# Attention pairs on TensorE: scores issued together with the values of the pair ahead, and a new order at the end of the output projection

## The chip, the cores and the metric

The kernel runs on one core of a Trainium2 chip. The metric is device time in microseconds (us) of one execution; the figure for a kernel is the median of several executions. TensorE (PE in the profile) has a separate sequencer for weight loads (PEld), which can run beside a matmul; VectorE is DVE, ScalarE is ACT, GpSimd is POOL, and SP issues most DMAs. TensorE works strictly in the order in which its instructions were written.

## The reference

Two layers act on x (256 rows of 1024, float32), with a memory of 256 rows:

```
h = rms_norm(x, norm_g); proj = h @ w_in           # 1024 x 3584
oa = causal attention, 6 heads of 64   (qa, ka: rms_norm and rope)
ob = dilated attention, 6 heads of 64  (three patterns; for 256 rows one mask of log counts)
om = attention on the memory, 4 heads  (mkv = rms_norm(mem) @ w_mem_kv)
y = concat(oa * silu(a_g), ob * silu(b_g), om * silu(m_g))
x = x + y @ w_out                                  # 1024 x 1024
```

Everything is float32. The kernel splits each float32 operand of a large product in a high and a low part (fp32r) and adds three products.

## The kernel before

**Stages.** A layer runs through the projections mkv, mq, mg (memory side), bq, bk, bv, bg (dilated side), aq, ak, av, ag (causal side), and then the output projection. A projection has eight steps over the rows of the weights. The output projection has eight chunks of 128 rows of w_out, taken in the order e = 6, 7 (memory), 3, 4, 5 (dilated), 0, 1, 2 (causal), and four PSUM banks (128 rows of x by 512 columns). One chunk on one bank is called a part here: three matmuls, `out_products` (L658). A chunk e needs `yT[:, e]`, which the pair of heads e makes.

**Pairs of heads.** There are eight pairs in a layer: 0 and 1 of the memory side (e = 6, 7), 2 to 4 of the dilated side (e = 3, 4, 5), 5 to 7 of the causal side (e = 0, 1, 2). `pair_of_heads` (L300) is a generator for one pair. It turns q and k (four transposes), computes the scores of two heads (L319: eight TensorE instructions on half the rows of the array each, written 64*128 in the profile), starts a softmax for each head (`head`, L345; after it three or four transposes, L374, and a copy to pT), computes the values (L336: eight instructions on half the columns, written 128*64), then y (L341), and the two parts of yT (L575, L576). Scores, softmax, transposes and values of a pair depend on each other in that order.

**Order.** The order on TensorE is fixed when the program is written out. A counter `clock` adds an assumed cost for each matmul (L109). After each step of a projection, and after each part, `poll` (L124) resumes the generators whose due time has come. So the work of the pairs stands in visits between steps of the large products. A generator asks to be resumed some units of the counter later (`D_QK` 2.5 after the transposes, `D_SOFTMAX` 5 after the scores, `D_PT` 2.5 after the transposes of the softmax) and `until` puts it off by 0.3 while a condition fails. `live` holds the conditions: scores in the order of pairs with at most three softmax tiles in use, values in the order of pairs with one output bank, and `ready`, which is due times for the projections of the values and of the gates. `finish` (L136) moves the counter on, without any matmul, until a pair is done.

**End of a layer.** `last` (L671) keeps the weights of e = 1 and 2. When the other six chunks are through all banks, each bank takes e = 1 and then e = 2, and is added to x (L682). The next layer's products stand behind this.

Of the kernel before, what the change touches and what calls it, by code (L numbers as in the profile page):

```python
# [16 lines left out]
P = 128  # L17
T = 256
# [13 lines left out]
D_NORM, D_MEM, D_QK, D_SOFTMAX, D_PT, D_EVAC = 8, 1, 2.5, 5, 2.5, 4  # L32
D_FIRST_MEM, D_NEXT_MEM, D_PAIR, D_HEAD = 1, 3, 2, 1
WARM = 7

WHOLE = 2
NEG = -1e30
# [29 lines left out]
def hybrid_kernel(ctx: ExitStack, tc: tile.TileContext, x, mem, mem_t, gains, w_in, w_out, w_mem_kv, qk_g, const, out):  # L67
# [73 lines left out]
    def until(cond):  # L141
        while not cond():
            yield 0.3
# [125 lines left out]
    def normed(accs, n, dsts, tables, scale=None):  # L269
# [25 lines left out]
                                            op=ALU.mult))  # L295
        return rest

    live = dict(pr=0, pT=0, o=0, heads=0, pairs=0, s=0, t=0, v=0)

    def pair_of_heads(qn, kn, pair, masks, v, gate, ready, finished):  # L300

        ps = work()
        for t in range(NT):
            transpose(ps[:, t * P:(t + 1) * P], qn[:, t, pair * P:(pair + 1) * P])
            transpose(ps[:, 256 + t * P:256 + (t + 1) * P], kn[:, t, pair * P:(pair + 1) * P])
        qkT = sp.tile([P, 2, T], F32, tag="qkT", name="qkT", bufs=SLOTS)
        nc.scalar.copy(qkT.rearrange("p c t -> p (c t)"), ps)
        me = live["pairs"]
        live["pairs"] += 1
        yield D_QK  # L310
        yield from until(lambda: live["s"] == me and live["pr"] + 2 <= PR_BUFS)
        live["s"] += 1
        live["pr"] += 2
        scores = [work() for _ in range(2)]
        spans = [slice(0, 2 * P), slice(2 * P, 4 * P)] if masks is None else [slice(0, P), slice(P, 3 * P)]
        for t in range(NT):
            for j in range(2):
                q, k = (qkT[j * HD:(j + 1) * HD, c] for c in range(2))
                mm(scores[j][:, spans[t]], q[:, t * P:(t + 1) * P], k[:, 0:spans[t].stop - spans[t].start])  # L319
        pTs = []  # L320
        for j in range(2):
            rest = head(2 * me + j, scores[j], spans, masks, pTs)
            spawn(rest, next(rest))
        yield D_SOFTMAX
        yield from until(lambda: len(pTs) == 2)
        yield D_PT
        yield from until(lambda: live["v"] == me and live["o"] < O_BUFS and max(ready.values()) <= clock[0])
        live["v"] += 1
        live["o"] += 1
        o = o_p.tile([P, T], F32, tag="o", name="o")  # L330
        late = slice(0, T) if masks is None else slice(P, T)
        n = 2 * T if masks is None else T + P
        for t, to in ((0, slice(0, T)), (1, late)):
            for j in range(2):
                h = 2 * pair + j
                mm(o[j * HD:(j + 1) * HD, to], v[:, t, h * HD:(h + 1) * HD], pTs[j][:, t * T:n if t else T],  # L336
                   start=t == 0, stop=t == 1, shared=j)
        live["pT"] -= 2
        yield 0.6
        y = sp.tile([P, T], F32, tag="y", name="y", bufs=2)  # L340
        nc.vector.scalar_tensor_tensor(y, o, 0.5, gate[:, pair], op0=ALU.mult, op1=ALU.mult)  # L341
        live["o"] -= 1
        finished(y)

    def head(me, s, spans, masks, pTs):  # L345

        pr = sp.tile([P, 512], F32, tag="pr", name="pr", bufs=PR_BUFS)
        nm = sp.tile([P, NT], F32, tag="nm", name="nm", bufs=4)
        sums = sp.tile([P, NT], F32, tag="sums", name="sums", bufs=4)
        if masks is None:  # L350
            nc.vector.tensor_reduce(nm, s.rearrange("p (t k) -> p t k", t=NT), axis=AX.X, op=ALU.max, negate=True)
            for t in range(NT):
                nc.scalar.activation(pr[:, spans[t]], s[:, spans[t]], AF.Exp, bias=nm[:, t:t + 1],
                                     accum_out=sums[:, t:t + 1])
            blocks = [0, 2 * P, P, 3 * P]
        else:
            for t in range(NT):
                nc.vector.tensor_tensor_reduce(out=pr[:, spans[t]], in0=s[:, spans[t]], in1=masks[t], scale=-1.0,  # L358
                                               scalar=3e38, op0=ALU.add, op1=ALU.min, accum_out=nm[:, t:t + 1])
                nc.scalar.activation(pr[:, spans[t]], pr[:, spans[t]], AF.Exp, scale=-1.0, bias=nm[:, t:t + 1],  # L360
                                     accum_out=sums[:, t:t + 1])
            blocks = [0, P, 2 * P]
        rinv = sp.tile([P, NT], F32, tag="rinv", name="rinv", bufs=4)
        nc.vector.reciprocal(rinv, sums)
        for t in range(NT):
            nc.scalar.activation(pr[:, spans[t]], pr[:, spans[t]], AF.Copy, scale=rinv[:, t:t + 1])  # L366
        yield D_SOFTMAX + D_HEAD * (me % 2)
        yield from until(lambda: live["t"] == me and live["pT"] < PT_BUFS)
        live["t"] += 1
        live["pT"] += 1  # L370
        n = P * len(blocks)
        ps = work()
        for i, c in enumerate(blocks):
            transpose(ps[:, i * P:(i + 1) * P], pr[:, c:c + P])  # L374
        live["pr"] -= 1
        pT = sp.tile([P, 512], F32, tag="pT", name="pT", bufs=PT_BUFS)
        nc.scalar.copy(pT[:, :n], ps[:, :n])  # L377
        pTs.append(pT)
# [122 lines left out]
    for l in range(DEPTH):  # L501
# [71 lines left out]
        def finished(y, e, yT=yT, done=done):  # L573
            done.add(e)
            nc.scalar.copy(yT[0][:, e], y)  # L575
            nc.vector.tensor_tensor(yT[1][:, e], y, yT[0][:, e].bitcast(F32), op=ALU.subtract)  # L576

        def start_heads(pairs, e0, qn, kn, masks, v, gate, ready, delay=D_NORM):
            for pair in range(pairs):
                spawn(pair_of_heads(qn, kn, pair, masks, v, gate, ready,  # L580
                                    lambda y, e=e0 + pair: finished(y, e)), delay + D_PAIR * pair)


        qn, kn, kv, gate = head_tiles(256, 512)
# [46 lines left out]
        for kind, e0 in ((2, 3), (0, 0)):  # L631
            if kind == 2:
                masks = [cst[:, C_DIL:C_DIL + 128], cst[:, C_DIL + 128:C_DIL + 384]]
            else:
                masks = [cst[:, C_CAUSAL + 128:C_CAUSAL + 256], cst[:, C_CAUSAL:C_CAUSAL + 256]]
            if l + 1 < DEPTH and kind == 0:
                mem_xs = xm_tiles()
                spawn(next_mem(mem_xs, gT[:, 24 + 8 * l:32 + 8 * l]), D_FIRST_MEM)
            qn, kn, v, gate = head_tiles(384, 384)
            ready = dict(v=1e9, gate=1e9)  # L640
            for i, dst in ((0, qn), (1, kn)):
                accs = run(project(xs, weights(), 384))
                normed(accs, 384, [dst[:, t] for t in range(NT)],
                       [[tab[:, kind + i, c, t] for t in range(NT)] for c in range(2)])()
            start_heads(3, e0, qn, kn, masks, v, gate, ready)
            for t, acc in enumerate(run(project(xs, weights(), 384))):
                nc.scalar.copy(v[:, t], acc)
            ready["v"] = clock[0] + D_EVAC
            gates(run(project_t(xs, weights(), 256)), gate[:, 0:2])
            gates(run(project_t(xs, weights(), 128)), gate[:, 2:3])  # L650
            ready["gate"] = clock[0] + D_EVAC


        whole_banks = [(t, c, 512) for t in range(NT) for c in (0, 512)]
# [8 lines left out]
        for c in ("om", "ob", "oa"):  # L663
            for k, _, w in weights():
                e = e_rows[c][0] + k
                finish(lambda: e in done)
                if c == "om" and k == 0:
                    banks = {(t, half): acc_p.tile([P, 512], F32, tag="acc", name="acc")
                             for t in range(NT) for half in range(2)}
                if e in (1, 2):  # L670
                    last.append((e, w))  # L671
                    continue
                for part in whole_banks:
                    out_products(e, w, *part)
                    poll()
        for t, c, n in whole_banks:
            for e, w in last:
                out_products(e, w, t, c, n)
            step = n // 2 if l == DEPTH - 1 and (t, c) == whole_banks[-1][:2] else n
            for a in range(c, c + n, step):  # L680
                cols = slice(a, a + step)
                nc.vector.tensor_tensor(x_sb[:, t, cols], banks[t, c // 512][:, a % 512:a % 512 + step],  # L682
                                        x_sb[:, t, cols], op=ALU.add)
                if l == DEPTH - 1:
                    nc.sync.dma_start(out[t * P:(t + 1) * P, cols], x_sb[:, t, cols])
# [30 lines left out]
```

## Time and profile before

| | us |
|---|---|
| median of three executions | 292.31 (291.97 to 292.39) |
| the profiled execution | 292.05 |
| its span, first to last instruction | 290.3 |
| outside the span | 1.75 |
| TensorE busy | 285.2 of 290.3 |

The granted clock of TensorE is 1.00 in the whole span, its higher level. Times in the rows are in us from the start of the span. A row of the timeline has the start, the length from the first start to the last end, the engine, the line, the operation and how many instructions are merged in it; the end of a matmul is modelled and reaches into the next one, so the price of a piece of work is read from start to start.

### The profile page before, as it was taken

How to read it: one execution, taken by the hardware profiler on the slowest of the kernel's cores; microseconds unless marked ns; L12 is line 12 of the kernel's file. 1: busy time of each engine (PE TensorE's matmuls, PEld its weight loads, DVE VectorE, ACT ScalarE, POOL GpSimd, SP SyncE). 2: the span in 40 equal slices, each digit the busy share in tenths (PEclk: the TensorE clock that was granted, in tenths of full speed). 3: DMA queues.
4: the chain of work that ended last, by engine and by line, in shares of the span. 5: the costliest groups of instructions: out<-in, count | busy, mean ns of one | idle time of the engine just before them, and what ended most of it. 6: DMA issues, size and time to landing. Idle time of an engine off the chain costs nothing.

```text
span 290.3 us, 4972 instructions
## 1 busy us (share of the span) xinstructions
PE 285.2 (98%) x1810; PEld 250.7 (86%) x1810; DVE 205.2 (71%) x461; ACT 200.1 (69%) x446; POOL 54.3 (19%) x72
## 2 busy tenths in 40 slices
PE   8999999999999999999999999999999999999994
PEld 5799999889989999877788999989899899987773
DVE  1798999793677996764676577979655699765313
ACT  2899678876789638985367555868578865698600
POOL 0003993200003220000020069503000113000000
PEclk9999999999999999999999999999999999999999
DMA  7999575627335237538025828360913624920003
GB/s 234 391 368 365 211 214 166 168 56 269 111 93 163 71 121 250 215 143 288 2 76 181 252 76 230 135 183 0 325 31 105 231 64 153 342 74 21 3 0 145
DMA packets 32793, 47.33 MB, mean 163 GB/s; under 512 B 1280, under 2 KB 27648, under 8 KB 32768
## 3 DMA queue, kind: packets, MB, share of 16 engines
q1 hardware_dynamic: 32336, 46.22, 48.6%
q10 hardware_dynamic: 432, 0.79, 0.8%
q8 instruction: 14, 0.23, 0.3%
q14 instruction: 11, 0.09, 0.1%
HBM read 45.96 MB, written 1.05 MB: 162 GB/s over the span
## 4 chain that ended last, share of the span: by engine, by line
PE 97%; DMA 1%; DVE 0%; SPq 0%; DVEq 0%; issue 0%
PE acc L110 79%; PE wk L113 8%; PE wk L110 5%; PE o L110 5%; DMA memT<-in_mem_t_dram 1%; PE o L113 0%; DVE x_sb L682 0%; SPq L469 0%; DVE whole L515 0%; DVEq L712 0%; DVEq L515 0%
## 5 line engine op out<-in xcount | busy, mean ns | idle before, releaser
L450 DVE TENSOR_TENSOR lo<-raw,hi 128x768 fp32r<-128x768 f32 (+1 forms) x90 | 95.6, 1088 | 30.8 <-ACT hi L449 30.7
L449 ACT CAST hi<-raw 128x768 fp32r<-128x768 f32 (+1 forms) x90 | 82.9, 935 | 30.8 <-PE acc L110 22.9
L110 PE MATMUL acc<-hi,xmh 128*128 128x384 f32 (+2 forms) x252 | 67.4, 349 | 0.0
L110 PE MATMUL acc<-lo,xmh 128*128 128x384 f32 (+2 forms) x252 | 63.7, 335 | 0.0
L110 PE MATMUL acc<-hi,xml 128*128 128x384 f32 (+2 forms) x252 | 63.7, 335 | 0.0
L155 POOL TENSOR_TENSOR hrs<-ms,mhalf 128x6 f32<-128x6 f32 (+1 forms) x24 | 30.1, 1260 | 118.1 <-DVE ms L154 117.6
L110 PEld LDWEIGHTS acc<-hi,xmh 128*128 128x128 f32 x252 | 42.6, 189 | 5.0 <-issue 3.3
L110 PEld LDWEIGHTS acc<-lo,xmh 128*128 128x128 f32 x252 | 45.0, 188 | 1.2
L110 PEld LDWEIGHTS acc<-hi,xml 128*128 128x128 f32 x252 | 44.9, 188 | 1.1
L110 PE MATMUL acc<-hi,yT 128*128 128x512 f32 x128 | 41.0, 402 | 0.0
L110 PE MATMUL acc<-xmh,hi 128*128 128x256 f32 x128 | 29.7, 293 | 0.0
L110 PE MATMUL acc<-xml,hi 128*128 128x256 f32 x128 | 28.4, 283 | 0.0
L110 PE MATMUL acc<-xmh,lo 128*128 128x256 f32 x128 | 28.4, 283 | 0.0
L110 PEld LDWEIGHTS acc<-hi,yT 128*128 128x128 f32 x128 | 23.0, 188 | 4.8 <-issue 0.7
L360 ACT ACTIVATE pr<-pr,nm 128x128 f32<-128x128 f32 (+1 forms) x48 | 21.3, 446 | 7.8 <-DVE nm L358 7.8
L366 ACT ACTIVATE pr<-pr,rinv 128x128 f32<-128x128 f32 (+1 forms) x64 | 25.8, 463 | 0.0
L110 PE MATMUL acc<-lo,yT 128*128 128x512 f32 x64 | 25.0, 391 | 0.0
L110 PEld LDWEIGHTS acc<-xmh,hi 128*128 128x128 f32 x128 | 20.9, 191 | 0.7 <-issue 0.7
L110 PEld LDWEIGHTS acc<-xml,hi 128*128 128x128 f32 x128 | 21.0, 191 | 0.0
L110 PEld LDWEIGHTS acc<-xmh,lo 128*128 128x128 f32 x128 | 21.0, 191 | 0.0
L377 ACT COPY pT<-wk 128x384 f32<-128x384 f32 (+1 forms) x32 | 15.5, 503 | 5.9 <-PE wk L113 5.9
L358 DVE CUSTOM_DVE_ANT_0 pr<-wk,cst 128x128 f32<-128x128 f32 (+1 forms) x48 | 14.3, 353 | 3.3 <-PE wk L110 3.3
(83 smaller groups left out, 357.6 us busy)
## 6 DMA issues: line engine op xcount, KB each, us to landing
raw<-in_w_in_dram SPq DMA_DIRECT2D x24, 768.0 KB, 5.3
raw<-in_w_in_dram SPq DMA_DIRECT2D x7, 1024.0 KB, 5.5
raw<-in_w_out_dram SPq DMA_DIRECT2D x6, 1024.0 KB, 5.0
raw<-in_w_in_dram SPq DMA_DIRECT2D x6, 512.0 KB, 3.7
raw<-in_w_out_dram SPq DMA_DIRECT2D x4, 512.0 KB, 4.0
raw<-in_w_mem_kv_dram SPq DMA_DIRECT2D x2, 1024.0 KB, 5.3
raw<-in_w_mem_kv_dram SPq DMA_DIRECT2D x2, 512.0 KB, 6.8
x_sb<-in_x_dram SPq DMA_DIRECT2D x2, 512.0 KB, 7.3
```

Source lines behind the costliest of these rows:

```text
L110: pe(nc.tensor.matmul(out, a, b, start=start, stop=stop), us)
L113: pe(nc.tensor.transpose(out, a, ident), 0.109)
L155: pin(nc.gpsimd.tensor_tensor(dst, ms, mhalf[:, :n], op=ALU.pow))
L358: nc.vector.tensor_tensor_reduce(out=pr[:, spans[t]], in0=s[:, spans[t]], in1=masks[t], scale=-1.0, scalar=3e38, op0=ALU.add, op1=ALU.min, ...
L360: nc.scalar.activation(pr[:, spans[t]], pr[:, spans[t]], AF.Exp, scale=-1.0, bias=nm[:, t:t + 1], accum_out=sums[:, t:t + 1])
L366: nc.scalar.activation(pr[:, spans[t]], pr[:, spans[t]], AF.Copy, scale=rinv[:, t:t + 1])
L377: nc.scalar.copy(pT[:, :n], ps[:, :n])
L449: pin(nc.scalar.copy(hi, raw))
L450: pin(nc.vector.tensor_tensor(lo, raw, hi.bitcast(F32), op=ALU.subtract))
```

## The change

A pair that has its pT no longer issues its values at once. It puts a function into `pending`, and waits until the next pair takes it, the next pair has issued its scores, or 14 units have passed. The next pair, once it may issue its scores, waits up to 5 units for a pending pair ahead (on the dilated and causal sides except the last causal pair; not on the memory side but for its first pair), issues its scores, and then the pending values right behind them. The last causal pair (`alone`, e = 2) doesn't wait, and its delays are 1.5 and 1 units shorter. The due time of the gates is no condition for the values any more. In the output projection the program no longer waits for e = 1 and 2 when their weights are taken; the end goes through banks 0, 1, 2 with e = 1, then banks 0, 1, 2 with e = 2, then bank 3 with both, and waits for each e only there, polling after each part.

```diff
--- before.py
+++ after.py
@@ -32,6 +32,7 @@
 D_NORM, D_MEM, D_QK, D_SOFTMAX, D_PT, D_EVAC = 8, 1, 2.5, 5, 2.5, 4
 D_FIRST_MEM, D_NEXT_MEM, D_PAIR, D_HEAD = 1, 3, 2, 1
 WARM = 7
+D_PARTNER, D_SCORES = 5, 14
 
 WHOLE = 2
 NEG = -1e30
@@ -295,9 +296,10 @@
                                             op=ALU.mult))
         return rest
 
+    pending = {}
     live = dict(pr=0, pT=0, o=0, heads=0, pairs=0, s=0, t=0, v=0)
 
-    def pair_of_heads(qn, kn, pair, masks, v, gate, ready, finished):
+    def pair_of_heads(qn, kn, pair, masks, v, gate, ready, finished, alone):
 
         ps = work()
         for t in range(NT):
@@ -309,6 +311,8 @@
         live["pairs"] += 1
         yield D_QK
         yield from until(lambda: live["s"] == me and live["pr"] + 2 <= PR_BUFS)
+        late = clock[0] + (D_PARTNER if masks is not None and not alone or pair == 0 else 0)
+        yield from until(lambda: live["v"] >= me or me - 1 in pending or clock[0] >= late)
         live["s"] += 1
         live["pr"] += 2
         scores = [work() for _ in range(2)]
@@ -318,31 +322,45 @@
                 q, k = (qkT[j * HD:(j + 1) * HD, c] for c in range(2))
                 mm(scores[j][:, spans[t]], q[:, t * P:(t + 1) * P], k[:, 0:spans[t].stop - spans[t].start])
         pTs = []
+        if me - 1 in pending:
+            pending.pop(me - 1)()
         for j in range(2):
-            rest = head(2 * me + j, scores[j], spans, masks, pTs)
+            rest = head(2 * me + j, scores[j], spans, masks, pTs, D_SOFTMAX - 1.5 * alone)
             spawn(rest, next(rest))
-        yield D_SOFTMAX
+        yield D_SOFTMAX - 1.5 * alone
         yield from until(lambda: len(pTs) == 2)
-        yield D_PT
+        yield D_PT - alone
         yield from until(lambda: live["v"] == me and live["o"] < O_BUFS and max(ready.values()) <= clock[0])
-        live["v"] += 1
-        live["o"] += 1
-        o = o_p.tile([P, T], F32, tag="o", name="o")
-        late = slice(0, T) if masks is None else slice(P, T)
-        n = 2 * T if masks is None else T + P
-        for t, to in ((0, slice(0, T)), (1, late)):
-            for j in range(2):
-                h = 2 * pair + j
-                mm(o[j * HD:(j + 1) * HD, to], v[:, t, h * HD:(h + 1) * HD], pTs[j][:, t * T:n if t else T],
-                   start=t == 0, stop=t == 1, shared=j)
-        live["pT"] -= 2
+        outs = []
+
+        def values():
+            live["v"] += 1
+            live["o"] += 1
+            o = o_p.tile([P, T], F32, tag="o", name="o")
+            late = slice(0, T) if masks is None else slice(P, T)
+            n = 2 * T if masks is None else T + P
+            for t, to in ((0, slice(0, T)), (1, late)):
+                for j in range(2):
+                    h = 2 * pair + j
+                    mm(o[j * HD:(j + 1) * HD, to], v[:, t, h * HD:(h + 1) * HD], pTs[j][:, t * T:n if t else T],
+                       start=t == 0, stop=t == 1, shared=j)
+            live["pT"] -= 2
+            outs.append(o)
+
+
+        pending[me] = values
+        late = clock[0] + (0 if alone else D_SCORES)
+        yield from until(lambda: outs or live["s"] > me + 1 or clock[0] >= late)
+        if not outs:
+            pending.pop(me)()
+        o = outs[0]
         yield 0.6
         y = sp.tile([P, T], F32, tag="y", name="y", bufs=2)
         nc.vector.scalar_tensor_tensor(y, o, 0.5, gate[:, pair], op0=ALU.mult, op1=ALU.mult)
         live["o"] -= 1
         finished(y)
 
-    def head(me, s, spans, masks, pTs):
+    def head(me, s, spans, masks, pTs, delay):
 
         pr = sp.tile([P, 512], F32, tag="pr", name="pr", bufs=PR_BUFS)
         nm = sp.tile([P, NT], F32, tag="nm", name="nm", bufs=4)
@@ -364,7 +382,7 @@
         nc.vector.reciprocal(rinv, sums)
         for t in range(NT):
             nc.scalar.activation(pr[:, spans[t]], pr[:, spans[t]], AF.Copy, scale=rinv[:, t:t + 1])
-        yield D_SOFTMAX + D_HEAD * (me % 2)
+        yield delay + D_HEAD * (me % 2)
         yield from until(lambda: live["t"] == me and live["pT"] < PT_BUFS)
         live["t"] += 1
         live["pT"] += 1
@@ -578,7 +596,7 @@
         def start_heads(pairs, e0, qn, kn, masks, v, gate, ready, delay=D_NORM):
             for pair in range(pairs):
                 spawn(pair_of_heads(qn, kn, pair, masks, v, gate, ready,
-                                    lambda y, e=e0 + pair: finished(y, e)), delay + D_PAIR * pair)
+                                    lambda y, e=e0 + pair: finished(y, e), e0 + pair == 2), delay + D_PAIR * pair)
 
 
         qn, kn, kv, gate = head_tiles(256, 512)
@@ -637,7 +655,7 @@
                 mem_xs = xm_tiles()
                 spawn(next_mem(mem_xs, gT[:, 24 + 8 * l:32 + 8 * l]), D_FIRST_MEM)
             qn, kn, v, gate = head_tiles(384, 384)
-            ready = dict(v=1e9, gate=1e9)
+            ready = dict(v=1e9)
             for i, dst in ((0, qn), (1, kn)):
                 accs = run(project(xs, weights(), 384))
                 normed(accs, 384, [dst[:, t] for t in range(NT)],
@@ -648,7 +666,6 @@
             ready["v"] = clock[0] + D_EVAC
             gates(run(project_t(xs, weights(), 256)), gate[:, 0:2])
             gates(run(project_t(xs, weights(), 128)), gate[:, 2:3])
-            ready["gate"] = clock[0] + D_EVAC
 
 
         whole_banks = [(t, c, 512) for t in range(NT) for c in (0, 512)]
@@ -663,7 +680,8 @@
         for c in ("om", "ob", "oa"):
             for k, _, w in weights():
                 e = e_rows[c][0] + k
-                finish(lambda: e in done)
+                if e not in (1, 2):
+                    finish(lambda: e in done)
                 if c == "om" and k == 0:
                     banks = {(t, half): acc_p.tile([P, 512], F32, tag="acc", name="acc")
                              for t in range(NT) for half in range(2)}
@@ -673,9 +691,15 @@
                 for part in whole_banks:
                     out_products(e, w, *part)
                     poll()
-        for t, c, n in whole_banks:
-            for e, w in last:
-                out_products(e, w, t, c, n)
+        ends = [(b, i) for i in range(2) for b in range(3)] + [(3, 0), (3, 1)]
+        for b, i in ends:
+            t, c, n = whole_banks[b]
+            e, w = last[i]
+            finish(lambda: e in done)
+            out_products(e, w, t, c, n)
+            poll()
+            if i == 0:
+                continue
             step = n // 2 if l == DEPTH - 1 and (t, c) == whole_banks[-1][:2] else n
             for a in range(c, c + n, step):
                 cols = slice(a, a + step)
```

## Rows read from the trace of the kernel before

**Rows 1.** Busy time of each engine in two stretches, from the first full matmul to the end of the last: us of the stretch, then busy us and instructions of each engine, granted clock, DMA share, GB/s.

```profile
4.70:153.00 148.30, 148.29 (x925) 129.29 (x926) 113.81 (x249) 110.95 (x242) 29.30 (x36) 1.00 0.57 190
153.00:286.60 133.60, 133.59 (x873) 118.36 (x871) 90.13 (x207) 87.66 (x202) 24.31 (x30) 1.00 0.41 133
```

**Rows 2.** Timeline of TensorE around scores that stand alone between steps (first layer, pair 2).

```profile
67.49 0.40 PE L110 MATMUL acc<-xmh,lo 128*128 128x256 f32 x2
67.81 0.93 PE L110 MATMUL wk<-qkT 64*128 64x128 f32 x8
68.67 0.50 PE L110 MATMUL acc<-xmh,hi 128*128 128x256 f32 x2
69.01 0.40 PE L110 MATMUL acc<-xml,hi 128*128 128x256 f32 x2
69.25 0.40 PE L110 MATMUL acc<-xmh,lo 128*128 128x256 f32 x2
```

**Rows 3.** Timeline of TensorE around values that stand alone (first layer, pair 2).

```profile
80.70 0.51 PE L110 MATMUL acc<-hi,xml 128*128 128x384 f32 x2
81.05 0.51 PE L110 MATMUL acc<-lo,xmh 128*128 128x384 f32 x2
81.49 0.87 PE L110 MATMUL o<-pT,v 128*64 128x256 f32 x8
82.29 0.62 PE L110 MATMUL acc<-hi,xmh 128*128 128x384 f32 x2
82.75 0.51 PE L110 MATMUL acc<-hi,xml 128*128 128x384 f32 x2
```

**Rows 4.** Timeline of the weight loads of TensorE, second layer: values, the product behind them, scores, and the product behind those. In brackets is the idle time of the loader before the row.

```profile
221.44 0.63 PEld L110 LDWEIGHTS o<-pT,v 128*64 128x64 f32 x8 [0.25 <-issue]
222.24 0.30 PEld L110 LDWEIGHTS acc<-hi,xmh 128*128 128x128 f32 x2 [0.17 <-issue]
225.19 0.52 PEld L110 LDWEIGHTS wk<-qkT 64*128 64x128 f32 x8 [0.25 <-issue]
226.05 0.30 PEld L110 LDWEIGHTS acc<-hi,xmh 128*128 128x128 f32 x2 [0.33 <-issue]
```

**Rows 5.** Timeline of TensorE in the output projection of the first layer: values (pair 5) with transposes behind them, then scores (pair 7) with transposes behind them.

```profile
123.94 0.39 PE L110 MATMUL acc<-lo,yT 128*128 128x512 f32 x1
124.26 0.87 PE L110 MATMUL o<-pT,v 128*64 128x256 f32 x8
125.06 0.55 PE L113 MATMUL wk<-ident,pr 128*128 128x128 f32 x3
...
125.91 0.40 PE L110 MATMUL acc<-lo,yT 128*128 128x512 f32 x1
126.24 0.93 PE L110 MATMUL wk<-qkT 64*128 64x128 f32 x8
127.09 0.55 PE L113 MATMUL wk<-ident,pr 128*128 128x128 f32 x3
...
127.94 0.39 PE L110 MATMUL acc<-lo,yT 128*128 128x512 f32 x1
```

**Rows 6.** The same timeline later: one full part (two rows) and the start of the next, and three transposes that stand alone.

```profile
128.17 0.61 PE L110 MATMUL acc<-hi,yT 128*128 128x512 f32 x2
128.63 0.39 PE L110 MATMUL acc<-lo,yT 128*128 128x512 f32 x1
128.85 0.61 PE L110 MATMUL acc<-hi,yT 128*128 128x512 f32 x2
...
133.07 0.40 PE L110 MATMUL acc<-lo,yT 128*128 128x512 f32 x1
133.31 0.49 PE L113 MATMUL wk<-ident,pr 128*128 128x128 f32 x3
133.56 0.71 PE L110 MATMUL acc<-hi,yT 128*128 128x512 f32 x2
134.11 0.40 PE L110 MATMUL acc<-lo,yT 128*128 128x512 f32 x1
```

**Rows 7.** Timeline of TensorE, the scores of pair 4 in the first layer and in the second.

```profile
85.24 1.11 PE L110 MATMUL wk<-qkT 64*128 64x128 f32 x8
...
225.19 0.93 PE L110 MATMUL wk<-qkT 64*128 64x128 f32 x8
```

**Rows 8.** Timeline of all engines at the end of the second layer, where the last pair becomes yT.

```profile
277.98 0.87 PE L110 MATMUL o<-pT,v 128*64 128x256 f32 x8
...
278.78 0.74 PE L110 MATMUL acc<-hi,yT 128*128 128x512 f32 x2
278.90 0.42 DVE L341 SCALAR_TENSOR_TENSOR y<-o,gate 128x256 f32<-128x256 f32 x1 [5.32 <-PE o L110]
...
279.36 0.41 ACT L575 CAST yT<-y 128x256 fp32r<-128x256 f32 x1 [4.22 <-DVE y L341]
...
279.79 0.42 DVE L576 TENSOR_TENSOR yT<-y,yT 128x256 fp32r<-128x256 f32 x1 [0.47 <-ACT yT L575]
```

**Rows 9.** The same at the end of the first layer, where weights of the next layer are still split.

```profile
138.48 1.23 DVE L450 TENSOR_TENSOR lo<-raw,hi 128x1024 fp32r<-128x1024 f32 x1 [1.86 <-ACT hi L449]
138.99 0.30 PEld L110 LDWEIGHTS acc<-hi,yT 128*128 128x128 f32 x2 [0.17 <-issue]
...
139.62 0.42 DVE L341 SCALAR_TENSOR_TENSOR y<-o,gate 128x256 f32<-128x256 f32 x1
...
140.51 0.43 DVE L576 TENSOR_TENSOR yT<-y,yT 128x256 fp32r<-128x256 f32 x1 [0.47 <-ACT yT L575]
141.17 1.05 ACT L449 CAST hi<-raw 128x1024 fp32r<-128x1024 f32 x1 [0.69 <-PE acc L110]
```

**Rows 10.** Timeline of ACT after the scores of pair 7, first layer: the first exponential, and the four scalings that end the softmax of both heads.

```profile
127.53 0.40 ACT L360 ACTIVATE pr<-pr,nm 128x128 f32<-128x128 f32 x1 [0.15 <-DVE nm L358]
...
129.66 1.50 ACT L366 ACTIVATE pr<-pr,rinv 128x128 f32<-128x128 f32 x4
```

**Rows 11.** Timeline of ACT in the second layer: the last cast of a weight in the program.

```profile
270.84 1.04 ACT L449 CAST hi<-raw 128x1024 fp32r<-128x1024 f32 x1
```

## The prediction

> **What bounds the kernel now.** I read the busy time by stretch first. From 4.70 to 286.60 us TensorE is busy in 281.88 of 281.90 us [rows 1], at the full granted clock. So there is no data wait to remove, and nothing on DVE, ACT or the DMA queues matters unless it makes TensorE wait. What can move the time is TensorE's own cost, and the reader should look for time in which it passes as busy and does little. The weight loader shows it: in the steps of the large products it runs ahead, but it stands idle 0.25 us before the weights of scores or values, 0.33 us after scores and 0.17 us after values [rows 4]. These are the places where the array goes from 128*128 to a half-row or half-column shape or back. So each visit pays twice for the change of shape, beside its work. The price of a visit is read from start to start. Two 256-column matmuls take 0.24 us [rows 2], two of 384 columns 0.35 [rows 3], and two of 512 columns 0.46, with 0.68 for a part [rows 6]. Lone scores: the product before ends at 67.49 + 0.24 = 67.73, the one behind is at normal pace from 69.01 - 0.24 = 68.77, so they cost 1.04. Lone values: 82.75 - 0.35 - (81.05 + 0.35) = 1.00.
>
> **The order after the change.** No arithmetic is added or removed; only the order changes. I walked the generators by hand with the costs of L109 (used for the order alone). The walk gives each visit of before where the trace has it, for example the values of pair 5 seven parts into the output projection, held by the gates' due time. For after it gives in each layer:
> - Pair 1's values wait for pair 2's scores, during bg: one visit, with the transposes of pair 4 behind. Pair 3's scores wait five steps, from the end of bg into aq, until pair 2's values are pending: one visit. Likewise 3 with the scores of 4, 4 with the scores of 5 (the transposes of pair 7 behind), 5 with the scores of 6 after the sixth part. Five shared visits in a layer, ten in all.
> - Pair 7's scores go alone after part 15 (before: part 8), since the scores of 6 came later. Pair 6's values follow after part 20, alone, with both transposes of pair 7's softmax right behind. Pair 7's values follow after part 24 (before: part 21). So `finish` never moves the counter without work: e = 1 is done by part 21, e = 2 in the poll after the first part of e = 1.
>
> **What a shared visit saves.** Entry 0.08 (67.73 to 67.81), scores up to the next shape 0.85 (126.24 to 127.09 [rows 5]), values up to the next shape 0.80 (81.49 to 82.29), and 0.11 for refilling behind (82.29 to 82.75 is 0.46 where 0.35 is normal): 1.84 against 1.04 + 1.00 = 2.04. It saves 0.20. No row has scores followed by values. From below, the step from one to the other might cost no change of shape, which would spare some 0.2 more; from above, it might cost as much as the two changes that it replaces, and save nothing. I take the row that I have, scores followed by another shape, 0.85. The loader's idle time after scores (0.33) and before values (0.25) shows TensorE emptying at each change of shape. The Trainium skill, TensorEngine Tiling (Array Packing), section Key Properties, says the same: changing the tiling mode, not just the tile, drains TensorE. Row tiling to column tiling is such a change, so the rule speaks against a larger gain: one of four drains goes, not two.
>
> **Shared edges that are lost.** Some visits of before already border on transposes, which have the shape of the large products. Three transposes alone cost 134.11 - 0.46 - (133.07 + 0.23) = 0.35 [rows 6]. Values with three cost 125.91 - 0.46 - (123.94 + 0.23) = 1.28, so 0.07 less than apart; scores with three cost 127.94 - 0.46 - (125.91 + 0.23) = 1.34, 0.05 less. The scores of pair 3 lose such an edge (0.05), and in the visit of pairs 6 and 5 both lose one (0.12). The values of pair 1 and the scores of pair 5 had an edge, and their shared visits have one behind them again. The sum for a layer: 5 x 0.20 - 0.05 - 0.12 = 0.83, and + 0.10 for pair 6's values, which gain the edge and put six transposes in one run (0.07, and one re-entry of about 0.03): 0.93. Two layers: 1.86. The scores of pair 4 took 1.11 us in the first layer and 0.93 in the second [rows 7]: 0.18 of waiting behind the transposes of pair 3's softmax, one step earlier. These will now be four steps earlier, so the wait should go. Sum 2.04.
>
> **What is added.** TensorE now gets yT of e = 2 much later, and everything behind it in its queue (the rest of the end, then the next layer's mkv) waits if it is late. Its cover is three parts of e = 1, 3 x 0.68 = 2.04, and 0.11. In the second layer yT is whole at 279.79 + 0.42 = 280.21, 1.43 after TensorE left the values at 278.78 [rows 8]: hidden. If the cover were gone, it would cost these 1.43. In the first layer a split of the next layer's weights stands in front on DVE, and it took 140.51 + 0.43 - 138.99 = 1.95: just hidden. But the cast of the buffer that chunk e = 0 frees (141.17 in before [rows 9]) will now fall into the same moment, and its DVE half takes 1.23; in front of y it makes 1.43 + 1.23 = 2.66, up to 0.6 late. Bounds 0 and 0.6; I take 0.2, nearer to the row of the first layer, which is hidden. The earlier transposes of pair 7 are asked for 0.31 (its neighbour's transposes) + 5 x 0.68 + 0.09 + 0.90 = 4.7 us after its scores left TensorE. In before the first head's scalings were over 129.66 + 0.75 - 127.09 = 3.3 after, the second's at 4.1 [rows 10]: hidden, with about 1 us, the length of one cast. Values of pairs 1 to 4 come up to 12 us later or sooner, but their chunks are taken tens of us after; the later scores of pair 3 (4.5 us) push its softmax and nothing on TensorE, since the transposes' due times move with it. The bank adds of the end come nearer together, but the last bank is unchanged, and so is the tail behind it. The gates' due time falls out: the gates are written before the values in all cases of the walk. SP and POOL are not touched.
>
> **Sum.** 2.04 - 0.20 = 1.84 saved. The profiled execution, 292.05, would take 290.2; on the median, 0.26 above it, 290.5. I say 290.4.
>
> **Rivals.**
> - The step from scores to values costs as much as the two changes that it replaces. Then ten merges give nothing, the lost edges stay: -2 x (0.17 - 0.10) + 0.18 - 0.20 = -0.16, so about 292.5. For it: both shapes are partial, and no row shows them together. Against it: all changes seen cost much the same. 0.08. The same time comes out if the merges don't come about because due times miss; each miss costs 0.2 only, and the walk has one margin under 0.1 unit (pair 5 after part 6), worth 0.4 over both layers, which stays in the forecast.
> - The step needs no emptying, since the loader works on tiles beside each other: 10 x 0.2 more, 288.5. The skill's rule above is against it, and so is the equal idle time at each change. 0.05.
> - Slower: e = 2 is late. The end waits for yT behind casts on ACT and DVE, in both layers. It decides from a chain of 2.15 us on, and it makes the kernel slower only if it eats the 2.04 of the sum and 0.6 more, 1.3 us per layer, that is yT 3.5 us after the values. That is 1.43 and two casts of about 1.1. In the second layer no cast is left by then (the last is at 270.84 [rows 11]), which speaks against it; the shortened delays of the last pair could add to it, with a late softmax. 293.0. 0.06.
>
> **How the numbers follow.** The forecast has 0.81, with its own range 289.6 to 291.4: the bounds of the wait (0 to 0.6), half of either bound for the step. For 8 in 10 the range goes from 289.3 to 291.9; the rivals, 0.19, lie outside. About 0.2%, 0.58 us, is what a measurement can tell from no change. Faster by more than that is below 291.7: the forecast and the second rival, less a little of the forecast's upper end, 0.84. Same: the first rival and that end, 0.10. Slower 0.06.
>
> **What would show it.** The trace should have ten places where 64*128 is followed by 128*64 with no 128*128 between, the second starting about 0.85 after the first; the loader's idle time on issue should be less by one 0.25 for each. TensorE should stay busy from 4.7 us to the end. The walk is wrong if the values of pair 7 don't come 24 parts into the output projection. The forecast is wrong if the first part of e = 2 waits on DVE or ACT, if transposes after pair 6's values wait on ACT, or if the step from scores to values is near 0.65 or 1.05.

## The result, and the profile after

The changed kernel took 290.00 us (median of six, 289.74 to 290.69) where the kernel before took 292.03 beside it (291.47 to 292.39): ratio 0.9936, 95% interval 0.9920 to 0.9953, so 1.4 to 2.3 us less. The forecast was 290.4, with 1.84 saved. The profiled execution took 289.94, with a span of 288.1. Single executions far above the others (351 us in e2, 562 us in e7) are left out of the times below.

Busy time by stretch, columns as in [rows 1]:

```profile
4.70:152.00 147.30, 146.47 (x926) 129.07 (x927) 114.40 (x250) 110.22 (x242) 29.19 (x36) 1.00 0.58 192
152.00:284.50 132.50, 132.49 (x871) 118.40 (x869) 90.51 (x207) 87.28 (x202) 23.49 (x30) 1.00 0.41 132
```

TensorE is still always busy and at full clock; the 0.83 us missing in the first stretch lie at its start, where it waited for VectorE, and VectorE for the first DMA. So the time came out of busy time. The timeline of TensorE in the output projection of the first layer shows where: a shared visit, pair 6's scores with pair 5's values.

```profile
120.95 0.39 PE L111 MATMUL acc<-lo,yT 128*128 128x512 f32 x1
121.27 0.93 PE L111 MATMUL wk<-qkT 64*128 64x128 f32 x8
122.12 0.87 PE L111 MATMUL o<-pT,v 128*64 128x256 f32 x8
122.92 0.74 PE L111 MATMUL acc<-hi,yT 128*128 128x512 f32 x2
123.50 0.39 PE L111 MATMUL acc<-lo,yT 128*128 128x512 f32 x1
```

The values start 0.85 after the scores, the same as transposes did [rows 5], and the product follows 0.80 later, as after lone values [rows 3]. The whole visit costs 123.50 - 0.46 - (120.95 + 0.23) = 1.86; 1.84 was forecast, and apart they cost 2.04. In all ten shared visits the values start 0.85 or 0.86 after the scores. The loader's rows in the second layer (scores, values, product of the shared visit of pairs 3 and 2) answer to [rows 4]:

```profile
219.04 0.52 PEld L111 LDWEIGHTS wk<-qkT 64*128 64x128 f32 x8 [0.25 <-issue]
219.90 0.63 PEld L111 LDWEIGHTS o<-pT,v 128*64 128x64 f32 x8 [0.33 <-issue]
220.70 0.30 PEld L111 LDWEIGHTS acc<-hi,xmh 128*128 128x128 f32 x2 [0.17 <-issue]
```

Where four idle times stood (0.25, 0.33, 0.25, 0.17), there are three: one entry is gone.

The end of the first layer answers to [rows 9], here with the parts of TensorE:

```profile
138.79 0.87 PE L111 MATMUL o<-pT,v 128*64 128x256 f32 x8
139.59 0.74 PE L111 MATMUL acc<-hi,yT 128*128 128x512 f32 x2
139.71 0.42 DVE L359 SCALAR_TENSOR_TENSOR y<-o,gate 128x256 f32<-128x256 f32 x1 [1.35 <-PE o L111]
140.05 1.22 DVE L468 TENSOR_TENSOR lo<-raw,hi 128x1024 fp32r<-128x1024 f32 x1
...
141.18 0.42 DVE L594 TENSOR_TENSOR yT<-y,yT 128x256 fp32r<-128x256 f32 x1
...
141.79 0.63 PE L111 MATMUL acc<-hi,yT 128*128 128x512 f32 x2
```

Three parts of e = 1 start at 139.59, 140.41 and 141.10; the first of e = 2 starts at 141.79, without a wait. The split of the next layer's weights did fall into this moment, but behind y: it stood between y and the second half of yT, and yT was whole at 141.60, just in time.

The scores of pair 4 take 0.93 in the first layer too, where they took 1.11 [rows 7]:

```profile
92.85 0.93 PE L111 MATMUL wk<-qkT 64*128 64x128 f32 x8
```

For the sums below I cut every trace at the same work: the first scores of each layer (pair 0), and the add of the last bank. In the changed kernel these are the rows

```profile
39.90 0.73 PEld L111 LDWEIGHTS wk<-qkT 64*128 64x128 f32 x8 [0.25 <-issue]
...
178.79 0.73 PEld L111 LDWEIGHTS wk<-qkT 64*128 64x128 f32 x8 [0.25 <-issue]
```

```profile
284.52 0.76 DVE L706 TENSOR_TENSOR x_sb<-acc,x_sb 128x256 f32<-128x256 f32 x2 [0.67 <-PE acc L111]
```

The same work in the kernel before starts at 40.27, 180.23 and 286.63. "First" is from the first mark to the second, "second" from there to the third, both read in the one profiled execution of each kernel. Ratios are to executions of the kernel before that ran beside the kernel of the row.

| kernel | to the first mark | first | second | sum | ratio to before (95%) |
|---|---|---|---|---|---|
| before | 40.27 | 139.96 | 106.40 | 246.36 | 1 |
| changed | 39.90 | 138.89 | 105.73 | 244.62 | 0.9936 (0.9920 to 0.9953) |
| e8, the changed kernel again | 41.24 | 138.89 | 105.52 | 244.41 | 0.9927 (0.9898 to 0.9956) |
| e1, values one step after the scores | 41.15 | 140.45 | 106.57 | 247.02 | 1.0039 (1.0027 to 1.0052) |
| e2, the old end | 40.31 | 140.23 | 106.07 | 246.30 | 1.0024 (1.0002 to 1.0045) |
| e3, no sharing | 39.87 | 140.54 | 107.02 | 247.56 | 1.0033 (1.0016 to 1.0049) |
| e4, scores don't wait | 40.62 | 139.40 | 106.02 | 245.42 | 0.9961 (0.9949 to 0.9974) |
| e9, usual delays for the last pair | 41.14 | 140.22 | 106.86 | 247.08 | 1.0014 (0.9997 to 1.0032) |
| e6, all seven visits shared | 40.25 | 140.26 | 106.34 | 246.60 | 1.0027 (1.0016 to 1.0038) |
| e7, memory pairs shared, + 2.5 | 40.09 | 142.13 | 107.06 | 249.19 | 1.0103 (1.0068 to 1.0139) |
| e10, memory pairs shared, + 1.2 | 39.92 | 138.69 | 105.33 | 244.02 | 0.9909 (0.9882 to 0.9936) |

The stretch to the first mark is the same program in all of them and spreads by 1.4 us, so it can't be put down to the change; TensorE waits there for data of the first DMAs. The layers repeat: 138.89 in both traces of the changed kernel. The 0.21 between its second layers is one wait inside the scores of memory pair 1 (1.35 us long, 1.13 in e8), which came once.

### The profile page after: what moved, and what is told of

It is laid out like the page before. It is cut to its first block, busy times and chain, and to the rows that moved or that the text cites. A ratio compares the mean times of both kernels' runs of the same rounds, so it can differ in the third digit from the quotient of the medians.

```text
span 288.1 us, 4967 instructions
## 1 busy us (share of the span) xinstructions
PE 282.3 (98%) x1810; PEld 250.5 (87%) x1810; DVE 205.9 (71%) x461; ACT 199.0 (69%) x446; POOL 53.4 (19%) x72
## 3 DMA queue, kind: packets, MB, share of 16 engines
HBM read 45.96 MB, written 1.05 MB: 163 GB/s over the span
## 4 chain that ended last, share of the span: by engine, by line
PE 97%; DMA 1%; DVE 0%; SPq 0%; DVEq 0%; issue 0%
PE acc L111 79%; PE wk L114 8%; PE wk L111 5%; PE o L111 5%; DMA memT<-in_mem_t_dram 1%; PE o L114 0%; DVE x_sb L706 0%; SPq L487 0%; DVE whole L533 0%; DVEq L736 0%; DVEq L533 0%
## 5 line engine op out<-in xcount | busy, mean ns | idle before, releaser
L111 PE MATMUL acc<-hi,xmh 128*128 128x384 f32 (+2 forms) x252 | 66.6, 346 | 0.0
```

Source lines behind the costliest of these rows:

```text
L111: pe(nc.tensor.matmul(out, a, b, start=start, stop=stop), us)
```

## The experiments

Theory A is the prediction's: each shared visit spares one change of the array's shape. Theory B: the gain comes from the rest of the change, the new end of the layer and the sooner last pair. Sums are compared with e8's 244.41.

**e8_changed_again.** The changed kernel itself. 

> The changed kernel itself, beside the two others on one chip. Both theories: ratio to before 0.992 to 0.995. The spans from the first scores of one layer to the first of the next should repeat to a few hundredths of a us (138.9), while the stretch ahead of the first scores, which waits on the first DMAs, may differ by half a us or more.

It came out so: 290.18 us, with 138.89 for the first layer.

**e1_apart.** The values a step later, everything else as changed:

```diff
         pTs = []
-        if me - 1 in pending:
-            pending.pop(me - 1)()
```

> The values of the pair ahead come one step (or part) after the scores instead of right behind them; all waits, the new end and the order of everything else stay. Theory A (each shared visit spares one of four changes of the array's shape, about 0.2 us): all ten are lost, and the sixes of transposes split into threes; some 2.0 us slower than the changed kernel, about as the kernel before (ratio to before 0.998 to 1.002). Theory B (the gain comes from the other places: last pair sooner, end of the layer, values later): the time stays at the changed kernel's, ratio 0.993 to 0.995.

It took 292.84 us; the ratio, 1.0039, is a little above the range of theory A. The same visit as above, now with a part between (TensorE, first layer):

```profile
121.95 0.93 PE L111 MATMUL wk<-qkT 64*128 64x128 f32 x8
122.81 0.73 PE L111 MATMUL acc<-hi,yT 128*128 128x512 f32 x2
123.38 0.40 PE L111 MATMUL acc<-lo,yT 128*128 128x512 f32 x1
123.70 0.87 PE L111 MATMUL o<-pT,v 128*64 128x256 f32 x8
124.50 0.73 PE L111 MATMUL acc<-hi,yT 128*128 128x512 f32 x2
```

From the scores to the product behind the values it is 2.55, and with sharing 1.65 plus a part of 0.68: 0.22 lost by the step between alone. The second layer is 1.05 longer than e8's, five times 0.21. The first is 1.56 longer, but has a wait beside it: its six transposes behind pair 6's values run from 135.43 to 136.71, 0.65 longer than the changed kernel's (135.21 to 135.84):

```profile
135.43 1.53 PE L114 MATMUL wk<-ident,pr 128*128 128x128 f32 x6
136.71 0.71 PE L111 MATMUL acc<-hi,yT 128*128 128x512 f32 x2
```

So 0.91 there without the wait, and 1.96 in both layers, where some 2.0 was expected. The wait has the cause told under e3. The adjacency is worth 0.2 us a visit, with the rest of the order unchanged. This shows theory A.

Is it the change of shape that costs, or any break in the row of large products? The transposes have the full shape, and the changed kernel has six of them behind values:

```profile
134.09 0.39 PE L111 MATMUL acc<-lo,yT 128*128 128x512 f32 x1
134.41 0.87 PE L111 MATMUL o<-pT,v 128*64 128x256 f32 x8
135.21 0.88 PE L114 MATMUL wk<-ident,pr 128*128 128x128 f32 x6
135.84 0.71 PE L111 MATMUL acc<-hi,yT 128*128 128x512 f32 x2
136.39 0.40 PE L111 MATMUL acc<-lo,yT 128*128 128x512 f32 x1
```

That visit costs 136.39 - 0.46 - (134.09 + 0.23) = 1.61, and values with three transposes cost 1.28 [rows 5]. So three more cost 0.33 in the same run, and 0.35 as a visit of their own [rows 6]: a break without a change of shape costs 0.02, a tenth of what a shared visit spares.

**e3_end_only.** No sharing, the rest of the change kept:

```diff
-        late = clock[0] + (D_PARTNER if masks is not None and not alone or pair == 0 else 0)
+        late = clock[0]
...
-        if me - 1 in pending:
-            pending.pop(me - 1)()
...
-        late = clock[0] + (0 if alone else D_SCORES)
+        late = clock[0]
```

> The changed kernel without pending values: values go as soon as they are due, scores wait for nobody; the new end, the shorter delays of the last pair and the gates' due time stay out or in as in the change. No visit is shared. Theory A (adjacency): about as the kernel before, ratio 0.998 to 1.000, since only the run of six transposes (0.10 per layer) and pair 4's wait can be gained. Theory B (the gain comes from the new end and the sooner last pair): as the changed kernel, 0.993 to 0.995.

It took 293.08 us, ratio 1.0033, slower than either expectation. In both layers the six transposes behind pair 6's values wait. First layer, TensorE, then VectorE and ScalarE after the scores of pair 7:

```profile
131.51 1.53 PE L114 MATMUL wk<-ident,pr 128*128 128x128 f32 x6
132.79 0.71 PE L111 MATMUL acc<-hi,yT 128*128 128x512 f32 x2
```

```profile
126.88 1.23 DVE L466 TENSOR_TENSOR lo<-raw,hi 128x1024 fp32r<-128x1024 f32 x1 [1.66 <-PE wk L111]
128.02 0.28 DVE L374 CUSTOM_DVE_ANT_0 pr<-wk,cst 128x128 f32<-128x128 f32 x1
...
130.81 1.03 ACT L465 CAST hi<-raw 128x1024 fp32r<-128x1024 f32 x1
131.75 0.80 ACT L382 ACTIVATE pr<-pr,rinv 128x128 f32<-128x128 f32 x2
```

A split of weights (1.23) went ahead of the softmax on VectorE, and a cast (1.03) ahead of the second head's scalings on ScalarE. These scalings end 5.76 after the scores left TensorE (126.79 to 132.55), in the changed kernel 4.06 (130.49 to 134.55), so the 1 us of cover (other work of TensorE in the meantime) that the prediction gave the shortened delays was gone: 1.28 for the six where 0.63 is normal, 0.65 in each layer. Without these 1.30 the layers would take 246.26, the kernel before has 246.36. So the other parts of the change bring nothing of their own, and the sooner last pair costs where a split and a cast run into it. Theory B falls.

**e4_no_wait.** Four shared visits in both layers instead of ten:

```diff
-D_PARTNER, D_SCORES = 5, 14
+D_PARTNER, D_SCORES = 0, 14
```

> Scores don't wait for the pair ahead (D_PARTNER 0), so only the visits of pairs 2 and 1 and of pairs 5 and 4 are shared: four in both layers instead of ten. Theory A: per layer 0.15 + 0.20 + 0.08 us lost, perhaps the 0.18 of pair 4's scores too; 0.9 to 1.1 us slower than the changed kernel, ratio to before 0.9965 to 0.9980. Theory B: as the changed kernel, 0.993 to 0.995.

It took 290.89 us; the ratio is a little better than expected, but the layers are 1.01 longer than e8's, inside 0.9 to 1.1. The gain falls with the number of shared visits. The 0.18 of pair 4's scores, which the expectation left open, didn't come back, although the transposes of pair 3's softmax stand one step ahead of them again, as in the kernel before (TensorE, first layer):

```profile
82.53 0.82 PE L114 MATMUL wk<-ident,pr 128*128 128x128 f32 x6
...
84.32 0.93 PE L111 MATMUL wk<-qkT 64*128 64x128 f32 x8
```

So the six lost visits cost 1.01 where the expectation has 0.86 for them alone; what makes the 0.15 stays open.

**e2_old_end.** The end as before, with the shared visits:

```diff
-                if e not in (1, 2):
-                    finish(lambda: e in done)
+                finish(lambda: e in done)
...
-        ends = [(b, i) for i in range(2) for b in range(3)] + [(3, 0), (3, 1)]
+        ends = [(b, i) for b in range(4) for i in range(2)]
```

> Only the end of the output projection is as before: each bank takes e = 1 and then e = 2, and the program waits for both pairs when their weights are taken. One part (0.68 us) instead of three covers the way of the last pair through y and yT. Theory A (the new end pays only as a cover): TensorE waits before the first part of e = 2, 0.6 us in the second layer, where yT takes 1.44, and up to 1.2 in the first, where it takes 2.0; 1.2 to 1.8 us slower than the changed kernel, ratio to before 0.997 to 1.000. Theory B (the end is where the gain is made): 2 us or more slower. If neither (the cover isn't needed): ratio 0.9935.

It took 292.46 us, with a wide spread, 291.41 to 294.85; the ratio, 1.0024, lies outside the range of theory A, and by the times alone it is 2 us or more slower than the changed kernel, as theory B has it. So this time doesn't part the theories, e3 does. In the trace the layers are 1.34 and 0.55 longer, 1.89 in all. The loader shows the wait in the second part behind the last values, in the first layer and in the second:

```profile
141.04 0.19 PEld L111 LDWEIGHTS acc<-hi,yT 128*128 128x128 f32 x1 [0.50 <-ACT yT L593]
142.07 0.19 PEld L111 LDWEIGHTS acc<-hi,yT 128*128 128x128 f32 x1 [0.84 <-DVE yT L594]
...
281.28 0.19 PEld L111 LDWEIGHTS acc<-hi,yT 128*128 128x128 f32 x1 [0.50 <-ACT yT L593]
281.74 0.19 PEld L111 LDWEIGHTS acc<-hi,yT 128*128 128x128 f32 x1 [0.27 <-DVE yT L594]
```

First for the high part of yT, then for the low one. The first two parts behind the values take 2.62 and 2.07 here, and 1.51 in the changed kernel, so this wait is 1.11 + 0.56 = 1.67 of the 1.89, inside 1.2 to 1.8. One part of cover is not enough, and three are. The layers, 246.30, are back at the 246.36 of the kernel before: without the new end the sharing gains nothing.

**e9_usual_delays.** The last pair with the delays of the others:

```diff
-            rest = head(2 * me + j, scores[j], spans, masks, pTs, D_SOFTMAX - 1.5 * alone)
+            rest = head(2 * me + j, scores[j], spans, masks, pTs, D_SOFTMAX)
...
-        yield D_SOFTMAX - 1.5 * alone
+        yield D_SOFTMAX
...
-        yield D_PT - alone
+        yield D_PT
```

> The changed kernel with the usual delays for the last pair (its transposes 5 units after its scores, its values 2.5 after those). The shared visits stay. Its values then come after all three parts of e = 1, with nothing between them and the first part of e = 2, so TensorE waits the way through y and yT: 1.0 to 1.4 us in the second layer, 1.4 to 2.0 in the first, where weights are still split. Theory A: 2.4 to 3.4 us slower than the changed kernel, ratio to before 1.001 to 1.006, all of it in that one wait. If the sooner last pair doesn't matter: 0.9930.

It took 292.98 us, its layers are 2.67 longer. Timeline of TensorE, both layers:

```profile
142.18 0.87 PE L111 MATMUL o<-pT,v 128*64 128x256 f32 x8
144.02 0.96 PE L111 MATMUL acc<-hi,yT 128*128 128x512 f32 x2 [0.96 <-ACT yT L593]
```

```profile
282.42 0.87 PE L111 MATMUL o<-pT,v 128*64 128x256 f32 x8
284.25 0.96 PE L111 MATMUL acc<-hi,yT 128*128 128x512 f32 x2 [0.96 <-ACT yT L593]
```

The product comes 1.84 after the values and not 0.80, and its second half waits for the low part of yT. From the values to the second part behind them it is 2.87 in both layers, where the changed kernel has 1.62 and 1.61: 2.51 of the 2.67 stand in this wait, more than the sharing won. So "sooner" gains nothing, but the sharing, which delays pair 7's scores, can't do without it.

**e6_share_causal.** Two more visits shared: scores of memory pair 1 with the values of pair 0, scores of pair 7 with the values of pair 6. The shorter softmax delay, and in the same way those of the head and of pT, hold for the causal pairs 5, 6 and 7 (`quick`).

```diff
-        late = clock[0] + (D_PARTNER if masks is not None and not alone or pair == 0 else 0)
+        late = clock[0] + D_PARTNER
...
-        yield D_SOFTMAX - 1.5 * alone
+        yield D_SOFTMAX - 1.5 * quick
```

> All seven visits of a layer that can be shared are: pair 1's scores wait for pair 0's values, pair 7's for pair 6's, with the shorter delays for all three pairs of the causal side. Theory A: two more visits in a layer, 0.20 for the memory pairs and 0.08 to 0.15 for the last two; 0.5 to 0.7 us faster than the changed kernel, ratio to before 0.991 to 0.992. A wait eats it if the softmax isn't over when its transposes are asked for (some 0.5 each). Theory B: no gain over the changed kernel.

It took 292.89 us, a miss. Memory pair 1's transposes wait in both layers, here in the first:

```profile
60.33 0.51 PE L111 MATMUL acc<-lo,xmh 128*128 128x384 f32 x2
61.43 0.94 PE L114 MATMUL wk<-ident,pr 128*128 128x128 f32 x4 [0.59 <-ACT pr L385]
62.13 0.59 PE L111 MATMUL acc<-hi,xmh 128*128 128x384 f32 x2
```

They stand 1.45 between products (60.68 to 62.13); four of them take 0.35 in e10 below. The later scores met the normalisation of the dilated keys on VectorE, which went first (52.74 to 57.5). In the first layer e = 2 is late besides: the loader stands 0.62 for yT.

**e7_share_memory.** Only the memory visit added (`late` as in e6, but 0 for the last pair), and its softmax given 2.5 units more. 

> The changed kernel with one more shared visit in a layer: the scores of memory pair 1 wait for the values of pair 0, and its softmax has 2.5 units more until its transposes are asked for, since they waited about 1 us where the delay stayed at 5. Theory A: 0.2 to 0.25 us per layer less, 0.4 to 0.7 us faster than the changed kernel with the wait of 0.21 that its second layer shows there, ratio to before 0.991 to 0.993. If the softmax is still late, the gain is gone and the trace shows the transposes waiting on ACT. Theory B: no gain over the changed kernel.

It took 295.19 us, a worse miss: the whole chain behind moved, and the softmax of pair 4 met the normalisation of the causal keys. Its transposes stood in the first layer from 103.39 to 106.30, 2.91 where 0.58 is normal; other waits (gates on VectorE, yT) came along.

```profile
105.01 1.53 PE L114 MATMUL wk<-ident,pr 128*128 128x128 f32 x6 [1.46 <-ACT pr L384]
```

**e10_share_memory.** The same with one step more in place of 2.5 units:

```diff
-            rest = head(2 * me + j, scores[j], spans, masks, pTs, D_SOFTMAX - 1.5 * alone)
+            rest = head(2 * me + j, scores[j], spans, masks, pTs, D_SOFTMAX - 1.5 * alone + 1.2 * (masks is None and pair == 1))
```

> As e7_share_memory, but with 1.2 units more for the softmax of memory pair 1, one step of TensorE, in place of 2.5, which pushed later softmaxes into the normalisation of the causal keys on VectorE. Theory A: 0.2 us per layer less than the changed kernel if no transposes wait, ratio to before 0.991 to 0.9925; each wait on ACT that is left costs what the trace shows for it. If sharing on the memory side always meets VectorE's normalisation of the dilated keys, the wait of the memory pair stays, and it is 1 us or more slower than the changed kernel.

It took 289.62 us, ratio 0.9909, the fastest of all by its median. In TensorE's row order scores (52.49) and values (53.55) stand together, and the four transposes of memory pair 1 give way to the next product after 0.35, without a wait:

```profile
52.49 1.13 PE L111 MATMUL wk<-qkT 64*128 64x256 f32 x8
53.55 1.08 PE L111 MATMUL o<-pT,v 128*64 128x256 f32 x8
...
61.80 0.60 PE L114 MATMUL wk<-ident,pr 128*128 128x128 f32 x4
62.15 0.48 PE L111 MATMUL acc<-xmh,hi 128*128 128x256 f32 x2
```

Its layers are 0.20 and 0.19 shorter than e8's: the price of one change of shape again, at a visit that the change had left apart. The intervals of e10 and of the changed kernel overlap, so the timing alone doesn't part them; the spans by layer do, as far as one execution of each can.

## Why the prediction was right

- **The bound.** TensorE was busy throughout, and the time came out of busy time at the changes of shape, not out of a wait.
- **The order.** All five shared visits of a layer stand where the walk put them, in both layers, and pair 7's values come eight parts before the end, so after part 24.
- **The price.** No row had scores followed by values; the row taken for it (0.85) was measured as 0.85. The two bounds, no change of shape and two of them, are both out. So a direct change from half rows to half columns costs as much as one from half rows to the full shape, with 0.33 us of idle loader in either case. The Trainium skill, TensorEngine Tiling (Array Packing), section Key Properties, says that a change of tiling mode drains TensorE; the trace agrees, with 0.33 between these two. The rivals call the loader's idle time equal at each change; the rows have 0.17 to 0.33, so the price had to be read from start to start, as the sum did.
- **The sum.** 2.04 was worked out for the two layers without new waits: 1.11 and 0.93. Measured 1.07 (139.96 - 138.89) and 0.88 (106.40 - 105.52 in e8). e1 confirms the term of 0.20 per visit, and e4 has 1.01 for six. The 0.18 of pair 4's scores is in the 1.07; it went as forecast, but the reason given, the distance to the transposes ahead, doesn't hold alone, since e4 has the old distance and no wait.
- **The waits.** 0.20 was set for a late e = 2 in the first layer; it didn't come, since y went ahead of the split on VectorE, with 0.2 us to spare. In its place the profiled run has 0.21 in a place that I hadn't named, and that the two are of one size is luck. The bound of 0.6 was a little high: with the cover of 2.15 that the rivals use, 2.66 is 0.51 late. The covers were sized rightly: the wait was 1.67 in e2 where 1.2 to 1.8 was expected, and 2.51 in e9 where 2.4 to 3.4 was.
- **What was weak.** I called the sooner last pair hidden with about 1 us. That held in the changed kernel, where the second head's scalings ended at 134.55 and its transposes stood at about 135.5, but e1 and e3 show it gone as soon as a split (1.23) and a cast (1.03) run ahead of that softmax. The median fell by 2.03, within the interval's 1.4 to 2.3, and can't be split further: the stretch ahead of the first scores alone moves by more than the 0.2 between forecast and result.

## What to carry to other kernels

Where TensorE is always busy, look for idle time of its weight loader: in this kernel each change between full, half-row and half-column shapes showed up in it, and putting two small pieces together spared about 0.2 us, although one was of half rows and the other of half columns. Price it from start to start, and count edges that the pieces already share with work of the full shape. Such a move delays the chain behind it, so check the last consumer's cover and which instructions of VectorE and ScalarE the later softmax will meet: a step more or less decided between 0.4 us won and 4.8 lost.

## What was not expected

- The same program took 39.9 to 41.2 us to its first scores in different executions, a spread larger than the effect of several experiments; cutting the trace at equal work gave 138.89 us twice for the first layer.
- 2.5 units more for one softmax (e7) cost 4.8 us, though every engine but TensorE is busy for some 70% at most: what hurt was one late chain on VectorE and ScalarE, in which TensorE stood still.
